# Value products behind both transposes, full-identity column transposes, and a sink column copied by ScalarE, in a hybrid mLSTM and sliding-window layer

## The chip, the core and the metric

The kernel runs on one core of a Trainium2 chip. The metric is the device time in microseconds of one execution, the median of several runs. A core has a matrix engine (TensorE, PE in the profile, with PEld for its weight loads), VectorE (DVE), ScalarE (ACT), GpSimd (POOL), and SyncE (SP), whose queue issues most of the transfers. Each engine takes its instructions in order; instructions of different engines wait for each other by semaphores.

## What is computed

One layer over a prompt of 2048 tokens and a batch of 8 x 16 sample tokens: an input projection, a gated matrix-memory recurrence (mLSTM, 4 heads of 128), sliding-window attention with a learned sink per head (8 query heads, 2 key heads of 64, window of the own chunk of 64 and two before), an output projection with LayerNorm, and a feed-forward part with a causal convolution of width 3. The attention, cut to what matters here:

```python
def band_attend(q, k, v, mask, sinks):
    s = einsum('bnlkgd,bnskd->bnkgls', q, k) * (A_HEAD_DIM ** -0.5)
    s = where(mask, s, -inf)
    sink = sinks.reshape(A_KV_HEADS, A_GROUP)[None, None, :, :, None, None]
    mx = maximum(max(s, axis=-1, keepdims=True), sink)
    p = exp(s - mx)
    p = p / (sum(p, axis=-1, keepdims=True) + exp(sink - mx))
    return einsum('bnkgls,bnskd->bnlkgd', p, v)
```

and of the recurrence, per chunk:

```python
    inter = b + m[..., None]
    dmat = where(causal, b[..., :, None] - b[..., None, :] + li[..., None, :], -inf)
    mt = maximum(inter, max(dmat, axis=-1))
    s = einsum('bhld,bhsd->bhls', qc, kc) * exp(dmat - mt[..., None])
    num = w_inter[..., None] * einsum('bhld,bhde->bhle', qc, C) + einsum('bhls,bhse->bhle', s, vc)
```

## The kernel before

Tokens go in 17 tiles of 128 (16 of the prompt, one of the sample batch). The large products are dense streams on TensorE: the input projection (`i_product`, L704, and `i_direct`, L730), then the output projection (`group`, by `mm3`, L222 to L224), then the two feed-forward products (L1873, L2083). Full precision comes from splitting each operand into a high and a low part and adding three products; the split of weights is a ScalarE cast (L217) and a VectorE subtraction (L218), that of the output projection's input L896 and L897.

The recurrence and the attention of the prompt tiles don't have a stage of their own. They are three generators (`t_sample`, `m_chain`, `a_chain`) whose steps are put between the dense products while the input projection and then the output projection run. TensorE's order is written out in this way by hand; the other engines' orders are found by a scheduler from the program's order and its dependencies.

The planner is `Chains`. Each dense yield adds its cost in ns to a clock `t`. A step yields up to three numbers: its own cost, the delay until the chain may go on, and how many PSUM banks the next step wants. `weave` (L183) takes the next step of a chain when its delay is over and so many of the 5 banks should be free; each bank asked for by `bank` (L927) counts as busy for `HOLDS[name]` ns (L35), or 3500. So a changed number there moves steps of all chains among the dense products.

The attention of one tile (`swa`, L1271): a score step for each half of the heads (`scores`, L1291: products L1303 into psc, mask and row maximum on VectorE, L1307, sink copied into the column behind the scores by GpSimd, L1297), exponentials on ScalarE (L1315, with row sums), division as a reciprocal on VectorE (L1318) and scaling on ScalarE (L1320). Then comes the loop over key tiles kt (nk is 1 for tile 0 and 2 for the others), L1337: eight transposes of the probabilities (L1342 into two ppt banks), copied by ScalarE to pth (L1343), and, one turn of the loop later, the value products of the key tile before (L1348 into ppo, two column halves of 64, one for each key head). In the first turn the next tile's queries and keys are transposed as well (`swa_first`, L1258: pq L1240, pk L1242, splits L217 and L218 to qh, ql, kringh, kringl). At the end ScalarE copies ppo to mixa (L1355) and SyncE stores it.

The recurrence of one tile (`m_tile`, L1182): gate rows (`m_rows`: transposes pgr L1007 and L1008, scans on VectorE, a row M sent through DRAM and broadcast to wi by two GpSimd transfers, L1078 and L1080), a column transpose (`m_cols`, L1020: pcol, 36 rows of ay against a 36x36 identity), exponentials L1117 and L1122, scores (pscore L1128, pkt L1138), then the numerator and state products (pnum L1211 and L1213, pcu L1220). The norm (`m_norm`) is VectorE work from L1150 to L1159 with a copy mr on ScalarE (L1153), a power on GpSimd (L1160), a scaling of hn on ScalarE (L1166, `m_scaled`) and transposes pht (L1176, `m_out`).

`d_sums` (L840) prepares sums of down-projection weights for later in the same stretch: loads into txy, four VectorE operations (L850 to L853), and stores.

Of the kernel before, what the change touches and what calls it, by code (L numbers as in the profile page):

```python
# [14 lines left out]
P = 128  # L15
# [16 lines left out]
RING = 3  # L32

NBANKS = 5
HOLDS = {"pm": 6500, "pgr": 4000, "pnum": 5000, "ppo": 6500}  # L35

WB = 4

# [166 lines left out]
class Prog:  # L205
# [721 lines left out]
    def bank(self, shape, name):  # L927
        self.chains.ask(HOLDS.get(name, 3500))
        return self.tps.tile(shape, F32, name=name, tag="tb")

    def t_setup(self):
        nc, a, tp = self.nc, self.a, self.tp

        def ld(n):
            t = self.one("k_" + n, list(a[n].shape))
            nc.sync.dma_start(t, a[n])
            return t
        nc.sync.dma_start(self.ident, a["ident"])
        self.gb = ld("gb")
        self.mcau = ld("mcau")  # L940
        self.mswa = ld("mswa")
        self.seg = ld("seg")
        self.sink = ld("sink")
        self.sinkx = ld("sinkx")
        self.m0 = ld("m0")
        self.nsink = self.one("nsink", [P, 8])
        nc.vector.tensor_scalar_mul(self.nsink, self.sink, -1.0)
        nc.vector.tensor_scalar_mul(self.sink, self.sink, 8.0)
        self.gm = ld("gm")
        nc.vector.tensor_scalar_mul(self.gm, self.gm, 0.5)  # L950

        raw = self.work("kw", [36, MH])
        nc.sync.dma_start(raw, a["sel"])
        self.sel = self.one("sel", [36, MH], F32R)
        nc.vector.tensor_copy(self.sel, raw)
        self.hl = [self.one(f"hl{i}", [36, P], F32R) for i in range(2)]
        self.ay = [self.one(f"ay{i}", [36, P]) for i in range(2)]
        for i in range(2):
            nc.vector.memset(self.ay[i], 0.0)
            nc.vector.tensor_copy(self.hl[i], self.ay[i])  # L960
        self.kh, self.kl = [self.one(n, [P, RING, P], F32R) for n in ("kringh", "kringl")]
        self.kv = {}
        self.C = self.work("C", [P, MH, 129], bufs=2)
        nc.vector.memset(self.C, 0.0)

        self.M = self.row("M")
        self.mc = self.M[:, P:]
        nc.vector.memset(self.mc, 0.0)
# [51 lines left out]
    def m_cols(self, i):  # L1020

        nc = self.nc
        ps = self.bank([P, 36], "pcol")
        nc.tensor.transpose(ps, self.ay[i], self.ident[:36, :36])
        col = self.work("col", [P, 36], bufs=2)
        nc.vector.tensor_copy(col, ps)
        return col

    def m_emt(self, col):
# [241 lines left out]
    def swa(self, t):  # L1271
        nc = self.nc
        V = nc.vector
        if self.a_first is None:
            self.swa_first(t)
            yield 550, 4000, 2
        qh, ql = self.a_first
        self.a_first = None
        r = t % RING
        if t == 0:  # L1280
            slots, nk = [0], 1
            mask = self.mswa[:, :P]
            sel = slice(0, 1)
        else:
            slots, nk = sorted([(t - 1) % RING, r]), 2
            mask = self.mswa[:, P:] if slots[1] == r else self.mswa[:, :2 * P]
            sel = slice(slots[0], slots[1] + 1, slots[1] - slots[0])
        N = nk * P
        mix = self.work("mixa", [P, 4, P])

        def scores(j0):  # L1291

            sink, nsink = [x.rearrange("p (k j) -> p k j", k=2)[:, :, j0:j0 + 2] for x in (self.sink, self.nsink)]
            sc = self.work("sc", [P, 4, 2 * P + 4], bufs=2)
            mx, sm = [self.work(n, [P, 4], bufs=2) for n in ("amx", "asm")]
            w = lambda x: x.rearrange("p (k j) -> p k j", k=2)
            nc.gpsimd.tensor_copy(sc[:, :, N:N + 1].rearrange("p (k j) o -> p k (j o)", k=2), sink)  # L1297
            ps = [self.bank([P, 2, 2, P], "psc") for _ in range(2)]
            for j in range(2):
                for i, (q, k) in enumerate(((qh, self.kh), (qh, self.kl), (ql, self.kh))):  # L1300
                    for kvh in range(2):
                        rs = slice(64 * kvh, 64 * kvh + 64)
                        nc.tensor.matmul(ps[kvh][:, j, :nk], q[rs, j0 + j], k[rs, sel], start=i == 0, stop=i == 2)  # L1303
            for kvh in range(2):
                for j in range(2):
                    c = 2 * kvh + j
                    V.tensor_tensor_reduce(out=sc[:, c, :N], in0=ps[kvh][:, j, :nk].rearrange("p a b -> p (a b)"), in1=mask, scale=1.0, scalar=-3e38,  # L1307
                                           op0=ALU.add, op1=ALU.max, accum_out=mx[:, c:c + 1])

            V.scalar_tensor_tensor(w(mx), w(mx), -0.125, nsink, op0=ALU.mult, op1=ALU.min)  # L1310
            return sc, mx, sm

        def exps(sc, mx, sm):
            for j in range(4):
                nc.scalar.activation(sc[:, j, :N + 1], sc[:, j, :N + 1], AF.Exp, bias=mx[:, j:j + 1], scale=0.125, accum_out=sm[:, j:j + 1])  # L1315

        def divided(sc, mx, sm):
            V.reciprocal(sm, sm)  # L1318
            for j in range(4):
                nc.scalar.activation(sc[:, j, :N], sc[:, j, :N], AF.Copy, scale=sm[:, j:j + 1])  # L1320

        z = [scores(0)]
        yield 900, 3200, 2
        exps(*z[0])
        z.append(scores(2))
        yield 900, 3600
        exps(*z[1])
        divided(*z[0])
        if t + 1 < NPT and self.i_done > self.place(t + 1)[0]:
            self.a_load = self.swa_dma(t + 1)  # L1330
        yield 0, 3000
        divided(*z[1])
        scs = [x[0] for x in z]
        yield 0, 4200, 2 + 2 * (self.a_load is not None)

        po = pts = None
        for kt in range(nk + 1):  # L1337
            new = self.work("pth", [P, 2, 512], bufs=2) if kt < nk else None
            for kvh in range(2) if kt < nk else ():
                pp = self.bank([P, 512], "ppt")  # L1340
                for j in range(4):
                    nc.tensor.transpose(pp[:, j * P:(j + 1) * P], scs[j // 2][:, 2 * kvh + j % 2, kt * P:(kt + 1) * P], self.ident)  # L1342
                nc.scalar.copy(new[:, kvh], pp)  # L1343
            if kt:
                po = po or self.bank([P, 512], "ppo")
                for kvh in range(2):
                    w = self.kv[slots[kt - 1]][:, P + 64 * kvh:P + 64 * kvh + 64]
                    nc.tensor.matmul(po[64 * kvh:64 * kvh + 64], w, pts[:, kvh], start=kt == 1, stop=kt == nk)  # L1348
            pts = new
            if kt == 0 and self.a_load is not None:  # L1350

                self.swa_first(t + 1)
                self.chains.t += 550
            yield (860 if kt < nk else 0) + (1400 if kt else 0), 0 if kt == nk else 1500 if kt else 3000, 2 * (kt + 1 < nk) + (kt == 0)
        nc.scalar.copy(mix.rearrange("p a b -> p (a b)"), po)  # L1355
        self.mix_out(t, 4, mix)

# [828 lines left out]
```

## Time and profile before

| | us |
|---|---|
| three runs | 2321.00, 2317.24, 2315.28 |
| median | 2317.24 |
| the profiled execution | 2316.15 |
| its span in the trace | 2314.3 |
| mean granted TensorE clock | 0.996 of full speed |

The page gives for each engine the busy time, its share of the span and the number of instructions. A timeline row is start, duration, engine, line, operation, tile written and tiles read, shapes, and the count of instructions merged into the row; in brackets is the time for which the engine stood idle before it and what ended that. A row of a window table has, for a stretch, the busy time of PE, PEld, DVE, ACT and POOL with their instructions, the granted clock, the share of the DMA engines and GB/s. Matmuls overlap, so the distance of their starts counts, not their durations. The prompt tiles' chains run from about 300 to 870 us; up to 640 us the dense stream is the input projection, then it is the output projection.

### The profile page before, as it was taken

How to read it: one execution, taken by the hardware profiler on the slowest of the kernel's cores; microseconds unless marked ns; L12 is line 12 of the kernel's file. 1: busy time of each engine (PE TensorE's matmuls, PEld its weight loads, DVE VectorE, ACT ScalarE, POOL GpSimd, SP SyncE). 2: the span in 40 equal slices, each digit the busy share in tenths (PEclk: the TensorE clock that was granted, in tenths of full speed). 3: DMA queues.
4: the chain of work that ended last, by engine and by line, in shares of the span. 5: the costliest groups of instructions: out<-in, count | busy, mean ns of one | idle time of the engine just before them, and what ended most of it. 6: DMA issues, size and time to landing. Idle time of an engine off the chain costs nothing.

```text
span 2314.3 us, 39788 instructions
## 1 busy us (share of the span) xinstructions
PE 2281.9 (99%) x14293; PEld 2094.9 (91%) x14293; DVE 1808.1 (78%) x3075; ACT 1269.0 (55%) x2377; POOL 279.5 (12%) x509
## 2 busy tenths in 40 slices
PE   8999999999999999999999999999999999999998
PEld 8999989989877778999999999999999978888876
DVE  8777687787688888998788777678766786895987
ACT  5453466776766655555656555555555544444442
POOL 0001000000011212121002000013111200100200
PEclk9999999999999999999999999999999999999999
DMA  7888999999977757888778889978898776756743
GB/s 276 287 308 297 301 309 336 314 310 342 315 269 240 240 201 270 303 319 311 276 289 274 306 304 311 315 264 287 312 294 261 225 282 208 261 175 215 255 157 108
DMA packets 300166, 632.38 MB, mean 273 GB/s; under 512 B 47869, under 2 KB 141121, under 8 KB 299969
## 3 DMA queue, kind: packets, MB, share of 16 engines
q1 hardware_dynamic: 295296, 616.14, 77.9%
q0 software_dynamic: 3520, 10.56, 1.4%
q10 hardware_dynamic: 1152, 3.15, 0.4%
q8 instruction: 113, 1.85, 0.3%
q14 instruction: 85, 0.69, 0.1%
HBM read 458.11 MB, written 171.64 MB: 272 GB/s over the span
## 4 chain that ended last, share of the span: by engine, by line
PE 76%; DVE 5%; DMA 4%; issue 2%; ACT 1%; SPq 0%; POOL 0%; DVEq 0%; ACTq 0%; POOLq 0%
PE dps L1873 19%; PE fup L1873 19%; PE dps L704 7%; PE dps L2083 6%; PE fht L2083 6%; PE fup L2083 6%; PE dps L222 2%; PE dps L224 2%; PE dps L223 2%; PE ppo L1348 1%; PE psc L1303 1%; PE ppt L1342 1%; DVE w L218 1%; PE fht L1697 1%; DMA txy<-wdn 0%
## 5 line engine op out<-in xcount | busy, mean ns | idle before, releaser
L1873 PE MATMUL dps<-hh,uw 128*128 128x384 f32 (+1 forms) x1848 | 478.7, 328 | 2.0 <-DVE u L1904 2.0
L1873 PE MATMUL fup<-hh,uw 128*128 128x384 f32 (+1 forms) x1848 | 478.2, 328 | 1.5 <-ACT ua L1894 1.5
L1873 PEld LDWEIGHTS dps<-hh,uw 128*128 128x128 f32 x1848 | 330.5, 188 | 2.2 <-DVE u L1904 2.2
L1873 PEld LDWEIGHTS fup<-hh,uw 128*128 128x128 f32 x1848 | 330.0, 188 | 2.0 <-ACT ua L1894 1.9
L1930 DVE SCALAR_TENSOR_TENSOR cc<-u,cw,cc 128x768 f32<-128x768 f32 (+1 forms) x264 | 258.1, 978 | 64.9 <-ACT cc L1928 55.5
L1873 PE MATMUL fup<-hl,uw 128*128 128x384 f32 (+1 forms) x924 | 302.5, 327 | 1.7 <-DVE hl L218 1.7
L1873 PE MATMUL dps<-hl,uw 128*128 128x384 f32 (+1 forms) x924 | 302.8, 328 | 0.0
L704 PE MATMUL dps<-w,oh 128*128 128x256 f32 x1344 | 254.3, 284 | 0.7 <-DVE zev L777 0.7
L217 ACT CAST uw<-wraw 128x1024 fp32r<-128x1024 f32 x126 | 123.0, 979 | 223.8 <-PE dps L2083 120.1
L218 DVE TENSOR_TENSOR w<-wraw,w 128x1024 fp32r<-128x1024 f32 (+2 forms) x167 | 189.4, 1141 | 56.1 <-ACT w L217 48.9
L217 ACT CAST w<-wraw 128x1024 fp32r<-128x1024 f32 (+2 forms) x167 | 163.0, 985 | 107.3 <-PE dps L704 38.9
L704 PEld LDWEIGHTS dps<-w,oh 128*128 128x128 f32 x1344 | 210.5, 188 | 11.8 <-issue 8.1
L218 DVE TENSOR_TENSOR uw<-wraw,uw 128x1024 fp32r<-128x1024 f32 x126 | 142.4, 1131 | 65.7 <-ACT uw L217 65.5
L704 PE MATMUL dps<-w,ol 128*128 128x256 f32 x672 | 187.8, 279 | 0.0
L704 PE MATMUL dps<-oh,w 128*128 128x256 f32 x896 | 170.9, 285 | 6.6 <-ACT mr L1153 3.8
L1873 PEld LDWEIGHTS fup<-hl,uw 128*128 128x128 f32 x924 | 173.5, 188 | 2.4 <-DVE hl L218 2.3
L2083 PE MATMUL fup<-uw,fu 128*128 128x512 f32 x726 | 174.2, 396 | 0.6 <-DVE uw L218 0.6
L1873 PEld LDWEIGHTS dps<-hl,uw 128*128 128x128 f32 x924 | 173.8, 188 | 0.0
L2083 PEld LDWEIGHTS fup<-uw,fu 128*128 128x128 f32 x726 | 136.6, 188 | 34.1 <-DVE uw L218 1.1
L2083 PE MATMUL dps<-uw,fu 128*128 128x512 f32 x660 | 165.3, 396 | 1.1 <-DVE uw L218 1.1
L1928 ACT ACTIVATE cc<-u,cw 128x768 f32<-128x768 f32 (+1 forms) x132 | 132.2, 1002 | 57.8 <-DVE u L1910 28.5
L704 PEld LDWEIGHTS dps<-oh,w 128*128 128x128 f32 x896 | 142.2, 191 | 13.1 <-ACT mr L1153 4.1
(318 smaller groups left out, 4567.0 us busy)
## 6 DMA issues: line engine op xcount, KB each, us to landing
uw<-zw SPq DMA_DIRECT2D x176, 512.0 KB, 5.1
zw<-uw SPq DMA_DIRECT2D x88, 512.0 KB, 3.7
w<-zws SPq DMA_DIRECT2D x72, 512.0 KB, 6.2
wv<-wup SPq DMA_DIRECT2D x66, 512.0 KB, 5.0
wraw<-wi SPq DMA_DIRECT2D x65, 512.0 KB, 5.1
wraw<-zt SPq DMA_DIRECT2D x60, 512.0 KB, 4.3
wraw<-wdn SPq DMA_DIRECT2D x45, 512.0 KB, 4.3
wraw<-wo SPq DMA_DIRECT2D x40, 512.0 KB, 4.5
```

The lines of the kernel that those rows point to most:

```text
L217: nc.scalar.copy(hi, src)
L218: nc.vector.tensor_sub(lo, src, hi.bitcast(F32))
L222: mm(out, ah, bh, start=start, stop=False)
L223: mm(out, ah, bl, start=False, stop=False)
L224: mm(out, al, bh, start=False, stop=stop)
L704: mm(o, l, r, start=s in (1, 7) and c == k == i == 0, stop=k == 3 and i == 2, skip_group_check=True)
L1303: nc.tensor.matmul(ps[kvh][:, j, :nk], q[rs, j0 + j], k[rs, sel], start=i == 0, stop=i == 2)
L1342: nc.tensor.transpose(pp[:, j * P:(j + 1) * P], scs[j // 2][:, 2 * kvh + j % 2, kt * P:(kt + 1) * P], self.ident)
L1873: mm(ps, l[:, k], r[:, k], start=s in (1, 7) and k == 0 and i == 0, stop=k == 3 and i == 2, skip_group_check=True)
L1928: S.activation(c[:, v], u[:, 2:2 + n], AF.Identity, bias=w[3], scale=w[2])
L1930: V.scalar_tensor_tensor(c[:, v], u[:, i:i + n], w[i], c[:, v], op0=ALU.mult, op1=ALU.add)
L2083: mm(ps, l[:, k, c], r[:, k], start=s in (1, 4, 7) and u == 0 and k == 0 and i == 0, stop=u == nu - 1 and k == n - 1 and i == 2, skip_grou ...
```

## The change

Three edits. In `m_cols` the column transpose takes all 128 rows of a now 128x128 ay (zero but for the rows used before) against the whole identity, and the copy to col takes the 36 columns that are wanted. In `scores` the sink column is copied by ScalarE, after the row maxima, in place of GpSimd before the score products. In the loop over key tiles the value products come in one step behind the transposes of both key tiles, with other yields; and the planner's hold for ppo is 5000 in place of 6500.

```diff
-HOLDS = {"pm": 6500, "pgr": 4000, "pnum": 5000, "ppo": 6500}
+HOLDS = {"pm": 6500, "pgr": 4000, "pnum": 5000, "ppo": 5000}
...
-        self.ay = [self.one(f"ay{i}", [36, P]) for i in range(2)]
+        self.ay = [self.one(f"ay{i}", [P, P]) for i in range(2)]
         for i in range(2):
             nc.vector.memset(self.ay[i], 0.0)
-            nc.vector.tensor_copy(self.hl[i], self.ay[i])
+            nc.vector.tensor_copy(self.hl[i], self.ay[i][:36])
...
-        ps = self.bank([P, 36], "pcol")
-        nc.tensor.transpose(ps, self.ay[i], self.ident[:36, :36])
+        ps = self.bank([P, P], "pcol")
+        nc.tensor.transpose(ps, self.ay[i], self.ident)
         col = self.work("col", [P, 36], bufs=2)
-        nc.vector.tensor_copy(col, ps)
+        nc.vector.tensor_copy(col, ps[:, :36])
...
-            nc.gpsimd.tensor_copy(sc[:, :, N:N + 1].rearrange("p (k j) o -> p k (j o)", k=2), sink)
             ps = [self.bank([P, 2, 2, P], "psc") for _ in range(2)]
...
             V.scalar_tensor_tensor(w(mx), w(mx), -0.125, nsink, op0=ALU.mult, op1=ALU.min)
+            nc.scalar.copy(sc[:, :, N:N + 1].rearrange("p (k j) o -> p k (j o)", k=2), sink)
             return sc, mx, sm
...
-        po = pts = None
-        for kt in range(nk + 1):
-            new = self.work("pth", [P, 2, 512], bufs=2) if kt < nk else None
-            for kvh in range(2) if kt < nk else ():
+        pts = []
+        for kt in range(nk):
+            new = self.work("pth", [P, 2, 512], bufs=2)
+            for kvh in range(2):
                 pp = self.bank([P, 512], "ppt")
                 for j in range(4):
                     nc.tensor.transpose(pp[:, j * P:(j + 1) * P], scs[j // 2][:, 2 * kvh + j % 2, kt * P:(kt + 1) * P], self.ident)
                 nc.scalar.copy(new[:, kvh], pp)
-            if kt:
-                po = po or self.bank([P, 512], "ppo")
-                for kvh in range(2):
-                    w = self.kv[slots[kt - 1]][:, P + 64 * kvh:P + 64 * kvh + 64]
-                    nc.tensor.matmul(po[64 * kvh:64 * kvh + 64], w, pts[:, kvh], start=kt == 1, stop=kt == nk)
-            pts = new
+            pts.append(new)
             if kt == 0 and self.a_load is not None:
 
                 self.swa_first(t + 1)
                 self.chains.t += 550
-            yield (860 if kt < nk else 0) + (1400 if kt else 0), 0 if kt == nk else 1500 if kt else 3000, 2 * (kt + 1 < nk) + (kt == 0)
+            yield 860, 3000 if kt + 1 == nk else 1500, 1 if kt + 1 == nk else 2
+        po = self.bank([P, 512], "ppo")
+        for kt in range(nk):
+            for kvh in range(2):
+                w = self.kv[slots[kt]][:, P + 64 * kvh:P + 64 * kvh + 64]
+                nc.tensor.matmul(po[64 * kvh:64 * kvh + 64], w, pts[kt][:, kvh], start=kt == 0, stop=kt + 1 == nk)
+        yield 1400 * nk, 0
         nc.scalar.copy(mix.rearrange("p a b -> p (a b)"), po)
```

## The prediction

> **What bounds the kernel now.** I read the page's span and engine shares first, then who TensorE waited for in the stretch in which attention and the gated recurrence run (300 to 870 us), then TensorE, ScalarE and VectorE in order of time around the steps that the change touches.
>
> ```profile
> span 2314.3 us, 39788 instructions
> PE 2281.9 (99%) x14293; PEld 2094.9 (91%) x14293; DVE 1808.1 (78%) x3075; ACT 1269.0 (55%) x2377; POOL 279.5 (12%) x509
> ```
>
> TensorE is busy 99% of the span; it sets the time. A microsecond counts only if it is TensorE's own work or a gap in TensorE. Its gaps in that stretch are few:
>
> ```profile
> PE dps L704 <- ACT mr L1153: 3.8, 1, 3.8
> PE ppt L1342 <- ACT pth L1343: 1.6, 1, 1.6
> PE pht L1176 <- DVE ql L218: 1.0, 1, 1.0
> PE ppo L1348 <- ACT pth L1343: 0.6, 1, 0.6
> ```
>
> (columns: total us, times, longest). So there is about 7 us to win in gaps, and whatever the step's own products lose when they interrupt the dense stream.
>
> **TensorE's own work: packing the value products and padding the column transpose.** In order of time, a dense product starts every 0.23 us; what a step costs is the time from the last dense start before it to the second dense start after it, less two such intervals (0.47).
>
> ```profile
> 661.72 0.40 PE L224 MATMUL dps<-w,ol 128*128 128x512 f32 x1
> 662.05 0.25 PE L1024 MATMUL pcol<-ident,ay 36*128 36x36 f32 x1
> 662.23 1.08 PE L1348 MATMUL ppo<-pth,kva 128*64 128x512 f32 x4
> 663.58 0.39 PE L223 MATMUL dps<-w,oh 128*128 128x512 f32 x1
> ```
> ```profile
> 761.46 0.39 PE L223 MATMUL dps<-w,oh 128*128 128x512 f32 x1
> 761.69 0.40 PE L224 MATMUL dps<-w,ol 128*128 128x512 f32 x1
> 762.02 0.25 PE L1024 MATMUL pcol<-ident,ay 36*128 36x36 f32 x1
> 762.53 0.39 PE L223 MATMUL dps<-w,oh 128*128 128x512 f32 x1
> 762.76 0.40 PE L224 MATMUL dps<-w,ol 128*128 128x512 f32 x1
> 763.09 1.08 PE L1348 MATMUL ppo<-pth,kva 128*64 128x512 f32 x4
> 764.44 0.39 PE L223 MATMUL dps<-w,oh 128*128 128x512 f32 x1
> ...
> 766.47 0.40 PE L224 MATMUL dps<-w,ol 128*128 128x512 f32 x1
> 766.70 0.27 PE L1007 MATMUL pgr<-ident,g 128*4 128x128 f32 x1
> 767.16 0.39 PE L223 MATMUL dps<-w,oh 128*128 128x512 f32 x1
> ```
> ```profile
> 791.29 0.40 PE L224 MATMUL dps<-w,ol 128*128 128x512 f32 x1
> 791.53 1.04 PE L1342 MATMUL ppt<-ident,sc 128*128 128x128 f32 x8
> 792.49 1.08 PE L1348 MATMUL ppo<-pth,kva 128*64 128x512 f32 x4
> 793.50 0.50 PE L222 MATMUL dps<-w,oh 128*128 128x512 f32 x1
> 793.84 0.40 PE L223 MATMUL dps<-w,oh 128*128 128x512 f32 x1
> ```
>
> A column transpose alone: 762.53 - 761.69 - 0.47 = 0.37 us, though it streams only 36 columns. Value products of one key tile alone: 764.44 - 762.76 - 0.47 = 1.21. Both together: 663.58 - 661.72 - 0.47 = 1.39. Eight transposes with products behind: 793.84 - 791.29 - 0.47 = 2.08, so the transposes take 2.08 - 1.21 = 0.87. The two gate transposes, all 128 rows deep: 767.16 - 766.47 - 0.47 = 0.22, or 0.11 each.
>
> Before, a tile of tokens with two key tiles pays 2.08 + 1.39 = 3.47. After, it pays 0.87 for the second transposes, one column transpose and one group of both key tiles' products. The 128x128 column transpose I take at 0.11, the gate transposes' price; its other end is its old 0.37. The double group the trace doesn't show. Between transposes and dense work, one key tile took 793.50 - 792.49 = 1.01, so I take 1.21 + 1.01 = 2.22. Its ends are 2.42 (nothing saved) and 2.02 (it sheds the 0.20 between 1.21 and 1.01 a second time). Sum after 0.87 + 0.11 + 2.22 = 3.20: 0.27 saved, for the 15 tiles with two key tiles **-4.1 us** (from -7.1 to -1.1). Tile 0 and the sample batch keep one group; their transposes add under 0.6.
>
> A page of the Trainium skill speaks against the padding: TensorEngine Tiling (Array Packing), under Instruction Overhead, has each matmul cost about as much as 60 columns, so 128 columns instead of 36 would cost some 68 cycles more, an estimate from that page of under 1 us over the 17 transposes, in place of a gain. The same page, under Key Properties, says that a change of tiling mode drains TensorE; the row of 0.37 us for 36 rows beside 0.11 for 128 agrees with that second rule, and I go by the row.
>
> **An early gap that goes.** Once, VectorE stood at a weight sum whose load was late, with the statistics that release TensorE's next bank behind it:
>
> ```profile
> 325.20 0.69 DVE L850 TENSOR_TENSOR txy<-txy 128x512 f32<-128x512 f32 x1 [3.92 <-DMA txy<-wdn]
> 325.81 0.29 DVE L1150 BATCH_NORM_STATS2 bst<-pnum 128x6 f32<-128x128 f32 x1
> ```
> ```profile
> 330.30 0.58 PE L704 MATMUL dps<-oh,w 128*128 128x256 f32 x1 [3.85 <-ACT mr L1153]
> ```
> ```profile
> 326.00:330.00 4.00, 0.46 (x4) 0.24 (x3) 3.85 (x16) 1.37 (x3) 0.00 (x0) 0.98 0.78 231
> 330.00:334.00 4.00, 3.70 (x20) 3.70 (x21) 4.00 (x10) 2.86 (x9) 0.00 (x0) 0.59 1.09 333
> ```
>
> (windows: PE, PEld, DVE, ACT, POOL busy, then granted clock.) ScalarE's mr waits for L1150, and the copy that frees TensorE's bank stands behind mr. TensorE lost 3.85 us, and in the next 4 us its clock was 0.59: 0.41 x 4 = 1.6 more. In the changed kernel as built, VectorE's order at this place has L850 behind the whole chain L1150 to L1159, some 6 us later, when the load (landed by 325.2) is there. Nothing that TensorE needs stands behind it then. **-5.4 us**; the other end is 0, if the load meets something else.
>
> The Trainium skill, TensorE: Matmul & The Clock Gate, Part 1, says that an idle window of about 3.4 us halves the clock until a busy one has passed; the row with 0.59 agrees.
>
> The other three gaps (1.6 + 1.0 + 0.6) sit at pairs of steps which the change pulls apart or re-times; I take them as gone, **-3.2 us** (or 0).
>
> **What becomes late: the second half's division.** The steps' waits and bank needs are new, and so the planner puts them in another order. In the output-projection stage (640 to 870 us) the second score step now comes 15 dense products before the recurrence's numerator, where it came 30 before. Its division is therefore issued after the recurrence's norm. As built, in three of the tiles of that stage VectorE's reciprocal L1318 stands behind L1159, and ScalarE's scaling L1320 behind the norm's L1166, which waits for GpSimd. The first transposes of the probabilities need all four of these scalings. One such tile in the old order, with pnum at 745.65:
>
> ```profile
> 745.65 0.39 PE L1211 MATMUL pnum<-v,dt 128*128 128x129 f32 x2
> ```
> ```profile
> 754.84 0.16 DVE L1159 TENSOR_TENSOR mr<-mr,bmv 128x4 f32<-128x4 f32 x1
> ```
> ```profile
> 755.15 1.89 POOL L1160 TENSOR_TENSOR ms<-mr,mhalf 128x4 f32<-128x4 f32 x1 [6.48 <-DVE mr L1159]
> ```
> ```profile
> 753.19 1.04 PE L1342 MATMUL ppt<-ident,sc 128*128 128x128 f32 x8
> ```
> ```profile
> 746.67 1.71 ACT L1320 ACTIVATE sc<-sc,asm 128x256 f32<-128x256 f32 x4
> ...
> 757.08 1.28 ACT L1166 ACTIVATE hn<-hn,ms 128x128 f32<-128x128 f32 x4 [1.52 <-POOL ms L1160]
> ```
>
> The norm ended at 758.36, 12.7 after pnum. Four scalings (1.71) bring that to 14.4. The transposes are due 7.54 after pnum now and, with 15 more dense products between (15 x 0.23 = 3.5), 11.0 then; the eight would end at 11.7. A gap of 14.4 - 11.7 = 2.7. A later tile, with pnum at 812.37, sets the far end:
>
> ```profile
> 823.37 0.16 DVE L1159 TENSOR_TENSOR mr<-mr,bmv 128x4 f32<-128x4 f32 x1
> ```
>
> There L1159 came 11.0 after pnum against 9.2, so 4.5. I take 2.9 for each of three tiles, and 1.0 for one weight cast that stands between norm and scaling in one of them: **+9.7 us**, from 0 (scalings in time) to 14.5. Behind a gap here, all dense products wait, nothing else becomes late.
>
> In three others the norm is followed on ScalarE by up to three weight casts and only then by the copies of the probabilities. Such a run:
>
> ```profile
> 648.65 3.18 ACT L217 CAST w<-wraw 128x1024 fp32r<-128x1024 f32 x3
> ```
>
> 12.7 + 3.2 + 0.6 for a copy = 16.5 after pnum, while the column transpose that reuses the copied bank is due at 11.0 + 1.4 (transposes and the next tile's loads) + 12 x 0.23 + 0.4 = 15.6. **+3 us** in all, from 0 to 6.
>
> **The sink column.** 32 copies of 128x4 leave GpSimd for ScalarE. The nearest row there, an exponential of the same size:
>
> ```profile
> 662.56 0.20 ACT L1031 ACTIVATE emt<-col 128x4 f32<-128x4 f32 x1 [0.67 <-DVE col L1026]
> ```
>
> 0.2 us each, 0.4 a tile, in a queue that is 55% busy; in the built order they stand behind the copies that drain the second transposes, so that they wait for nothing late. I cost them at nothing; without that cover, in the same queue as the late scalings, they cost 32 x 0.2 = 6.4. On GpSimd, L1558 and the recurrence's two transfers lose an instruction ahead of them that waited for transposes; no gap of TensorE named those. The store of the attention output is issued some 2 us later in SyncE's queue; its reader is a later block. The zeroing of larger ay tiles happens once.
>
> **The sum** against the profiled execution's own 2316.15 us: -4.1 - 5.4 - 3.2 + 9.7 + 3.0 = 0.0. The median of the runs shown is 2317.24, 1.1 higher, well inside their spread. I forecast **2316 us**, no change; of this kernel 0.3% (7 us) is about what a measurement can tell from none.
>
> **The rivals.** (1) Faster: VectorE reaches L1159 sooner, as it has more dense time around it, and neither division nor copies are late. Then 2316.15 - 12.7 = 2303. For it: the sooner end of L1159 isn't bounded by TensorE. Against: the chain takes weight casts in between in every tile I looked at. (2) Slower: each of the three late divisions costs the 4.5 of the far row and, as a gap over 3.8 us did before, 1.6 us of halved clock; with 1 for the cast and 6 for the others: -12.7 + 3 x 6.1 + 7 = +12.6, 2329. It decides from L1159 at 11 us after pnum on. (3) The packing and padding do nothing: the double group costs 2.42, the padded transpose 0.37, so a tile pays 3.66, 0.19 more than now: +2.9 in place of -4.1, 2323. Against it stand the 1.01 and 0.11 rows.
>
> **How the numbers follow.** My forecast 0.53, (1) 0.25, (2) 0.16, (3) 0.06. Case (1) gives faster; (2) and a part of (3) give slower: faster 0.26, within 0.3% 0.54, slower 0.20. The forecast's own range, with the bounds of its terms, is 2309 to 2322. The range 2302 to 2326 takes in (1) and (3) and leaves out most of (2).
>
> **What would show it.** In the profile after: column transposes 128x128 costing 0.1 us; eight value-product records together in about 2.2; no gap at 326 us and no 0.59 clock behind it; in the waits, PE ppt L1342 on ACT sc (the scalings) with 5 to 14 us in total, all after 640 us. If that wait is missing, (1) holds and I am wrong by the whole 9.7; if the granted clock drops behind these waits, (2).

## The result and the profile after

| | before | changed |
|---|---|---|
| runs | 14 | 14 |
| median, us | 2316.36 | 2321.34 |
| lowest and highest, us | 2312.09, 2324.22 | 2314.04, 2324.79 |

The ratio is 1.0018, with a 95% interval of 1.0010 to 1.0027: slower by 4 us (2317.24 x 0.0018), less than the 7 us set as the bound of no change, but more than its interval. The changed kernel's profiled execution took 2314.04 us, the lowest of its 14. A second one, e1_again below, took 2320.04 and stands near the median, so the account of times uses both.

The page of the changed kernel, first lines:

```profile
span 2312.2 us, 39714 instructions
...
PE 2276.4 (98%) x14293; PEld 2093.5 (91%) x14293; DVE 1808.9 (78%) x3075; ACT 1270.4 (55%) x2409; POOL 268.0 (12%) x477
```

TensorE still sets the time, and again the gaps decide. Its waits from 300 to 870 us (columns: total us, times, longest):

```profile
PE ppt L1342 <- ACT sc L1320: 4.8, 2, 4.5
PE pht L1176 <- ACT hn L1166: 1.3, 3, 0.5
PE pnum L1211 <- issue: 1.3, 1, 1.3
```

These are the first three of ten rows. The wait for mr (3.8) and the wait for pth of 1.6 are gone; the late scalings that the prediction named head the list, but with one wait of 4.5 where it had three of 2.9. (Lines from 1302 on have moved by one or a few: the norm keeps L1150 to L1166, the value products are L1354.)

**TensorE's own work.** The changed kernel's timeline of TensorE, a double group of value products and a full column transpose:

```profile
716.90 0.27 PE L1024 MATMUL pcol<-ident,ay 128*128 128x128 f32 x1
717.01 1.03 PE L1342 MATMUL ppt<-ident,sc 128*128 128x128 f32 x8
...
721.36 0.39 PE L224 MATMUL dps<-w,ol 128*128 128x512 f32 x1
721.67 1.94 PE L1354 MATMUL ppo<-pth,kva 128*64 128x512 f32 x8
723.54 0.50 PE L222 MATMUL dps<-w,oh 128*128 128x512 f32 x1
723.88 0.40 PE L223 MATMUL dps<-w,oh 128*128 128x512 f32 x1
```

The column transpose takes 717.01 - 716.90 = 0.11 us, the double group 723.88 - 721.36 - 0.47 = 2.05. With 0.87 for the transposes a tile pays 3.03 where it paid 3.47, so 15 tiles save 6.6 us; this is an estimate from these rows, and the other undisturbed groups of the trace repeat them within 0.02 us.

**The early gap.** The changed kernel's VectorE, then TensorE's waits from 300 to 345 us, then its windows (PE, PEld, DVE, ACT, POOL busy, granted clock, DMA share, GB/s):

```profile
330.07 0.15 DVE L1159 TENSOR_TENSOR mr<-mr,bmv 128x4 f32<-128x4 f32 x1
330.14 0.68 DVE L850 TENSOR_TENSOR txy<-txy 128x512 f32<-128x512 f32 x1
```
```profile
307.05 0.33 PE L1302 MATMUL psc<-kringl,qh 64*128 64x128 f32 x2 [0.73 <-DVE kringl L218]
318.64 1.13 PE L1211 MATMUL pnum<-v,dt 128*128 128x129 f32 x8 [1.29 <-issue]
332.22 0.33 PE L1176 MATMUL pht<-ident,hn 128*128 128x128 f32 x1 [0.39 <-ACT hn L1166]
332.99 0.33 PE L1176 MATMUL pht<-ident,hn 128*128 128x128 f32 x1 [0.45 <-ACT hn L1166]
333.81 0.62 PE L1176 MATMUL pht<-ident,hn 128*128 128x128 f32 x2 [0.48 <-ACT hn L1166]
```
```profile
330.00:334.00 4.00, 2.68 (x19) 2.05 (x17) 2.90 (x6) 2.24 (x7) 1.36 (x1) 1.00 1.04 396
334.00:338.00 4.00, 4.00 (x21) 3.89 (x20) 2.77 (x5) 4.00 (x11) 0.00 (x0) 0.57 0.92 305
```

L850 stands behind L1159 and no longer waits, as foretold. But the five brackets add up to 3.3 us. The kernel before had the first two waits as well, though smaller: 0.26 us ahead of its numerator at 319.2 us, and for the keys

```profile
308.75 0.33 PE L1303 MATMUL psc<-kringl,qh 64*128 64x128 f32 x2 [0.50 <-DVE kringl L218]
```

With its gap of 3.85 that is 4.6 us, so the waits of this stretch fell by 1.3 us, not by 3.85. And 4 us with a clock of 0.57 come here too, only later.

**The late division.** The prediction's three tiles: the start of the numerator, L1159, the last scalings, and the transposes that need them, each from the changed kernel's timeline of that engine:

```profile
668.07 0.38 PE L1211 MATMUL pnum<-v,dt 128*128 128x129 f32 x2
...
679.09 1.31 PE L1342 MATMUL ppt<-ident,sc 128*128 128x128 f32 x8
...
734.12 0.38 PE L1211 MATMUL pnum<-v,dt 128*128 128x129 f32 x2
...
745.90 1.13 PE L1342 MATMUL ppt<-ident,sc 128*128 128x128 f32 x5 [0.33 <-ACT sc L1320]
...
801.50 0.38 PE L1211 MATMUL pnum<-v,dt 128*128 128x129 f32 x2
...
812.52 0.38 PE L1342 MATMUL ppt<-ident,sc 128*128 128x128 f32 x2
817.39 1.73 PE L1342 MATMUL ppt<-ident,sc 128*128 128x128 f32 x6 [4.49 <-ACT sc L1320]
```
```profile
675.73 0.16 DVE L1159 TENSOR_TENSOR mr<-mr,bmv 128x4 f32<-128x4 f32 x1
...
741.90 0.15 DVE L1159 TENSOR_TENSOR mr<-mr,bmv 128x4 f32<-128x4 f32 x1
...
813.37 0.15 DVE L1159 TENSOR_TENSOR mr<-mr,bmv 128x4 f32<-128x4 f32 x1
```
```profile
816.83 1.71 ACT L1320 ACTIVATE sc<-sc,asm 128x256 f32<-128x256 f32 x4
```

The transposes are due 11.0 us after pnum in all three (679.09 - 668.07, 812.52 - 801.50), as worked out. L1159 comes 7.7, 7.8 and 11.9 us after pnum, so two tiles lose 0 and 0.33, and the third 4.49. In the third, two of the eight transposes run on time, as they need none of the late scalings, and TensorE goes on as soon as the first of the four is done. Around that gap the clock falls:

```profile
816.00:820.00 4.00, 2.61 (x12) 2.31 (x13) 3.32 (x3) 3.59 (x7) 0.00 (x0) 0.50 0.89 271
820.00:824.00 4.00, 4.00 (x16) 3.15 (x16) 2.81 (x7) 1.59 (x6) 0.42 (x1) 0.69 0.62 231
```

The clock record has one stretch of 6.8 us at half speed here, from 815.7 us. Its first 1.7 us fall into the gap, where TensorE stands anyway; the 5.1 us behind the gap cost at most 2.6 us.

**Where the time went.** The start of the same dense product, found in both traces by its number in the stream, shows how far the changed kernel is ahead or behind. Differences against the profile before, by stretches of that profile; the third line is the 15 tiles' saving. The fourth is the gap with its half clock; it is measured against e5 below, whose TensorE runs the same instructions in the same order and waits only 0.55 us there. The two profiles lose 5.8 and 7.2 us against e5 in that stretch; with e5's 0.55 these are the values given:

```
us                          after (2314.04)   e1_again (2320.04)
0 to 50                          -2.9               +0.1
50 to 870, of this:              +1.9               +0.8
  value products, transposes     -6.6               -6.6
  gap at 818 and its clock       +6.3               +7.7
  all else                       +2.2               -0.3
870 to 960                       +2.2               +4.0
960 to the end                   -3.2               -1.0
sum                              -2.0               +3.9
```

The first line is the chance of the clock: the profile before has two stretches at half clock in its first 50 us (granted 0.93 there), e1_again has them too, the other profile has none (1.00). Of the +2.2 in "all else", 1.2 lie ahead of 300 us. The line 870 to 960, the first steps of the feed-forward part, nobody had foreseen.

### The profile page after: what moved, and what is told of

Same layout as the page of the kernel before. It is cut to its first block, busy times and chain, and to the rows that moved or that the text cites. A ratio compares the mean times of both kernels' runs of the same rounds, so it can differ in the third digit from the quotient of the medians.

```text
span 2312.2 us, 39714 instructions
## 1 busy us (share of the span) xinstructions
PE 2276.4 (98%) x14293; PEld 2093.5 (91%) x14293; DVE 1808.9 (78%) x3075; ACT 1270.4 (55%) x2409; POOL 268.0 (12%) x477
## 4 chain that ended last, share of the span: by engine, by line
PE 73%; DVE 6%; DMA 4%; ACT 2%; issue 2%; POOL 0%; SPq 0%; DVEq 0%; ACTq 0%; POOLq 0%
PE dps L1874 19%; PE fup L1874 19%; PE dps L2084 6%; PE fht L2084 6%; PE fup L2084 6%; PE dps L704 5%; PE dps L222 2%; PE dps L223 2%; PE dps L224 2%; DMA r<-zf 1%; PE ppt L1342 1%; PE ppo L1354 1%; DVE w L218 1%; DMA txy<-wdn 1%; ACT sc L1315 1%
## 5 line engine op out<-in xcount | busy, mean ns | idle before, releaser
L2084 PEld LDWEIGHTS dps<-uw,fu 128*128 128x128 f32 x660 | 123.9, 188 | 31.4 <-DVE uw L218 1.5
```

The costliest lines, as they stand in the source:

```text
L2084: mm(ps, l[:, k, c], r[:, k], start=s in (1, 4, 7) and u == 0 and k == 0 and i == 0, stop=u == nu - 1 and k == n - 1 and i == 2, skip_grou ...
```

## The experiments

Each stands beside runs of the kernel before on the same chip (medians 2316.4 to 2317.5 us). Theory D is the prediction's: the late division sets the gap at 818 us.

**e1: the changed kernel once more**, no edit, for a second profile.

> The changed kernel once more, for the trace of another execution. Theory D (late divisions: in three tiles of the output-projection stage ScalarE's scaling of the second score half stands behind the recurrence's norm): 2321 us again, and in an execution near that time the gaps of TensorE at the first probability transposes before ACT sc L1320 sum to 6 to 12 us after 640 us, with stretches of halved clock behind them (the profiled execution of 2314.04 had 4.8). Rival E (the time is lost elsewhere, in the feed-forward stage or at the start): these gaps stay at 5 us or less and the time stands at another place.

2319.99 us, ratio 1.0014 (1.0004 to 1.0024). The slowdown holds. The gap at 818 us is 5.34 us here, and with one of 0.34 the waits for scalings come to 5.7, just short of the 6 that D asked for. The mean granted clock of the 12 runs is 0.9950, of the 35 runs before 0.9959: 0.0009 x 2317 = 2.1 us of a mean difference of 3.1. So up to two thirds of the slowdown are time at half clock.

**e2: the second half's division first, in every tile.**

```diff
-        divided(*z[1])
+        with self.tc.high_priority():
+            divided(*z[1])
```

> The changed kernel with the second division issued at high priority, so that its reciprocal and its scalings stand ahead of the norm on VectorE and ScalarE; TensorE's order is unchanged. D: no wait of ppt for ACT sc above 1 us, 5 to 10 us faster than the changed kernel, 2311 to 2316 us. E: within 2 us of the changed kernel, 2319 to 2323.

2319.82 us, ratio 1.0008 (0.9995 to 1.0020), where D had 2311 to 2316. The wait for scalings is gone, the gap isn't. TensorE's waits of this run, 600 to 880 us:

```profile
PE pht L1176 <- ACT hn L1166: 7.3, 2, 6.5
```

The norm itself is now the late thing. So D in its simple form, that the order of division and norm is all, fell.

**e3: the column transposes alone, on the kernel before.**

```diff
-        self.ay = [self.one(f"ay{i}", [36, P]) for i in range(2)]
+        self.ay = [self.one(f"ay{i}", [P, P]) for i in range(2)]
...
-        nc.tensor.transpose(ps, self.ay[i], self.ident[:36, :36])
+        nc.tensor.transpose(ps, self.ay[i], self.ident)
```

> The kernel before with only the 128x128 column transposes. Its order of instructions on VectorE has the weight sum L850 behind the statistics at the place of the early gap, as in the changed kernel. My pricing: column transposes save 13 x 0.07 + 3 x 0.26 = 1.7 us, the gap of 3.85 us at 330 us and its 1.6 us of lost clock go: 2309 to 2313 us. Rival (128 columns in place of 36 cost more, and the gap comes back elsewhere): 2316 to 2318.

2315.36 us, ratio 0.9987 (0.9972 to 1.0001): 3 us faster in the middle, not certain, and between the two expectations. The early gap of 3.85 is gone here already, and the small waits for norms (1.3 us) stand in its place as in the changed kernel.

**e4: the value products alone, on the kernel before.**

```diff
-HOLDS = {"pm": 6500, "pgr": 4000, "pnum": 5000, "ppo": 6500}
+HOLDS = {"pm": 6500, "pgr": 4000, "pnum": 5000, "ppo": 5000}
...
+        po = self.bank([P, 512], "ppo")
+        for kt in range(nk):
+            for kvh in range(2):
+                w = self.kv[slots[kt]][:, P + 64 * kvh:P + 64 * kvh + 64]
+                nc.tensor.matmul(po[64 * kvh:64 * kvh + 64], w, pts[kt][:, kvh], start=kt == 0, stop=kt + 1 == nk)
+        yield 1400 * nk, 0
```

> The kernel before with only the value products behind both transposes, their yields and the hold of 5000; the sink stays on GpSimd, the column transpose at 36 rows. D: it has late divisions in four tiles and keeps the early gap, so it is slower than the changed kernel, 2322 to 2328 us. Rival S (the sink copies on ScalarE cost the time): faster than the changed kernel by 4 to 7, 2314 to 2317.

2323.52 us, ratio 1.0031 (1.0021 to 1.0042). The cheaper products alone make the kernel slower by 6 us, with the wait for scalings (4.8 us) and the early wait (3.3 us) both there.

**The theory after these.** In the tile of the gap, ScalarE has another instruction out of place. The changed kernel's ScalarE, then SyncE's issues:

```profile
786.32 0.19 ACT L1310 COPY sc<-k_sink 128x4 f32<-128x4 f32 x1
793.42 1.05 ACT L896 CAST oh<-xraw 128x1024 fp32r<-128x1024 f32 x1 [6.92 <-DMA xraw<-zmix]
794.38 0.58 ACT L1356 COPY mixa<-ppo 128x512 f32<-128x512 f32 x1
794.85 0.20 ACT L1310 COPY sc<-k_sink 128x4 f32<-128x4 f32 x1
798.37 0.51 ACT L1315 ACTIVATE sc<-sc,amx 128x257 f32<-128x257 f32 x1 [3.32 <-DVE amx L1309]
```
```profile
783.51 0.38 SPq L1170 DMA_DIRECT2D zmix<-mixm  x1
...
789.42 0.89 SPq L892 DMA_DIRECT2D xraw<-zmix  x2
```

The cast reads a block of mixes that the store at 783.51 completes; store and load take till 793.4. In the changed kernel the cast stands ahead of mixa and the exponentials; in the kernel before it stands behind them (801.73 and 804.64 us in the profile before). That the scheduler moved it because mixm comes earlier is likely, but not shown. VectorE stands too, at ol, the subtraction behind the cast (3.0 us). Theory X: this wait makes the tile late. Rival N: the gap is repaid elsewhere.

**e5: that one cast behind the exponentials.**

```diff
-        nc.scalar.copy(h, raw)
+        with self.tc.issue_after(self.exp_done) if (b, p) == (3, 0) else nullcontext():
+            nc.scalar.copy(h, raw)
...
-                nc.scalar.activation(sc[:, j, :N + 1], sc[:, j, :N + 1], AF.Exp, bias=mx[:, j:j + 1], scale=0.125, accum_out=sm[:, j:j + 1])
+                self.exp_done = nc.scalar.activation(sc[:, j, :N + 1], sc[:, j, :N + 1], AF.Exp, bias=mx[:, j:j + 1], scale=0.125, accum_out=sm[:, j:j + 1]).ins
```

> The changed kernel with one edge more: ScalarE's cast oh<-xraw of the output projection's fourth block (tokens 10 to 13, the first of its four casts) is held behind the exponentials of tile 14's first half. ScalarE's order up to that tile is the changed kernel's own. Theory X (the cast at the head of ScalarE's queue waits for the store of tile 13's mix and the load behind it, 5.9 + 4 us, with mixa and the exponentials behind it): the wait on xraw<-zmix ahead of the cast falls from 6.7-6.9 us to under 1, the TensorE gap of 4.5 to 5.3 us at 818 us and the 6.8 us window at half clock behind it are gone, and the time is 2320 less 5.0 less 3.4, about 2311 to 2314. Rival D (the second half's late division sets the gap): this tile's division also moves ahead of the norm here, so D too expects the gap gone; the next run tells them apart. Rival N (the gap is repaid by slack later, or the time lies elsewhere): gap gone, time 2318 to 2322 as before.

2311.96 us, ratio 0.9984 (0.9973 to 0.9996): faster than both kernels. The scheduler, given the edge, also put all four scalings ahead of the norm in this tile, so two things changed at once. L1159 came 11.9 us after pnum, no sooner than in the changed kernel. One wait of half a microsecond is left there:

```profile
818.50 1.21 PE L1177 MATMUL pht<-ident,hn 128*128 128x128 f32 x4 [0.55 <-ACT hn L1167]
```

**e6: all casts of that kind behind the exponentials** (the same edit without its condition).

> The changed kernel with each of the output projection's input casts (x_pair, all blocks) held behind the exponentials last emitted. In the tile at 818 us the cast now comes after the first half's exponentials, while three of the second half's four scalings still stand behind the norm, as in the changed kernel. Theory X: the gap at 818 us is gone (under 1 us), no half clock there, 2311 to 2315. Rival D (the late division): the gap stays at 4 to 5 us on ppt waiting for the scalings, 2318 to 2322. Elsewhere the edge changes the order of a few scalings, worth under 2 us either way.

2320.49 us, ratio 1.0020 (1.0008 to 1.0033): no gain, against X. TensorE's waits for scalings:

```profile
747.32 1.27 PE L1343 MATMUL ppt<-ident,sc 128*128 128x128 f32 x5 [2.41 <-ACT sc L1321]
...
815.54 0.33 PE L1343 MATMUL ppt<-ident,sc 128*128 128x128 f32 x1 [0.64 <-ACT sc L1321]
818.63 1.27 PE L1343 MATMUL ppt<-ident,sc 128*128 128x128 f32 x5 [2.76 <-ACT sc L1321]
```

In the old place the cast is behind and the division late: 0.64 + 2.76 = 3.4 us remain, which D alone makes. The edge moved other work in the tile at 747 us, where L1159 came 9.9 us after pnum in place of 7.8, and that tile, harmless until then, lost 2.41.

**e7: the sink copied by GpSimd again, in the changed kernel** and **e8: that, with the edge of e6.**

```diff
+            nc.gpsimd.tensor_copy(sc[:, :, N:N + 1].rearrange("p (k j) o -> p k (j o)", k=2), sink)
...
-            nc.scalar.copy(sc[:, :, N:N + 1].rearrange("p (k j) o -> p k (j o)", k=2), sink)
```

> The changed kernel with the sink column copied by GpSimd again, at the place it had before; value products and column transposes as changed. Theory X: the cast stands at the same place ahead of mixa and the exponentials, so the gap at 818 us stays at 4 to 6 us and the time is that of the changed kernel, 2318 to 2322. Rival S (32 copies of 0.2 us on ScalarE and their places cost part of the loss): 2313 to 2317, with ScalarE's exponentials in the score steps 0.4 us sooner and the gap under 4.

> The edge of the run before last (casts behind the exponentials) and the sink on GpSimd together. If the two edits do not meet, the time is that of the casts held behind alone within 2 us: 2311 to 2315 by theory X. If the sink column on ScalarE costs something by itself, 2 to 4 us below that. By D it stays at 2318 to 2322.

2321.53 us, 1.0024 (1.0011 to 1.0037), with a gap of 4.4, as X expected; and 2324.23, 1.0038 (1.0025 to 1.0051), above all that was expected of it. Neither is faster with the sink on GpSimd: that edit is not where the time went.

**e9: the value products alone with the one edge of e5**, and **e10: e5 once more.**

> The kernel before with the merged value products alone (as in e4_products) and the one edge of e5_cast_last: the first cast of the output projection's fourth block behind the exponentials of tile 14's first half. Theory X2 (two causes at one place: with that cast ahead the tile at 818 to 830 us has a gap of 4.4 to 6.5 us whichever way the division is ordered; with the cast behind it, 2.8 us where the division is late and under 0.6 where it isn't): here the cast is behind and the division ahead of the norm, so the gap of 4.79 us at 827 us goes, with its 3.4 us of half clock: 2323.5 less 8 = 2313 to 2317. The early gap at 330 us stays at 3.3 us. Rival N (chance of one chip): 2320 to 2326, as e4_products.

> The kernel of e5_cast_last once more, on the chip of this call. Theory X2: 2310 to 2314, 3 to 6 us under before, no TensorE gap over 1 us between 600 and 880 us. If its first result was chance: 2316 to 2320.

2315.76 us, 0.9989 (0.9977 to 1.0001), where e4 had 1.0031: one edge is worth 0.0042 x 2317 = 10 us. And 2310.55 us, 0.9978 (0.9967 to 0.9990): e5's gain holds, 5 us below before.

**e11: the sink on ScalarE alone, on the kernel before** (e7's edit the other way).

> The kernel before with the sink column copied by ScalarE behind the score step's minimum, alone. ScalarE's order of the exponentials, scalings, norms and casts is that of before in all 16 tiles. Expected: the time of before within 2 us, the gap at 330 us still there, no gap over 2 us between 600 and 880. Rival S (the copies on ScalarE cost): 3 to 6 us above before.

2317.88 us, ratio 1.0000 (0.9989 to 1.0011). The sink copies cost nothing that shows; the 3 us at least of rival S lie outside the interval. One detail missed: a wait of 2.5 us for pth at 658 us, 1.65 in the profile before.

**e12: the division first in tile 14 alone**, in the changed kernel; the cast stays ahead.

```diff
-        divided(*z[1])
+        with self.tc.high_priority() if t == 14 else nullcontext():
+            divided(*z[1])
```

> The changed kernel with the second half's division raised in priority in tile 14 alone: ScalarE's four scalings move ahead of the recurrence's norm in the one tile with the gap, the cast stays ahead of mixa and the exponentials, and nothing earlier on ScalarE changes place. Theory X2 (with the cast ahead the gap comes whichever way the division is ordered): a gap of 4 to 6.5 us near 818 us, now on the norm (pht waiting for hn) in place of the scalings, and 2317 to 2322. Rival D (the late division alone): no gap over 1 us there, 2310 to 2314, as e5_cast_last.

2315.94 us, ratio 1.0002 (0.9992 to 1.0011): between the two expectations. The gap came as X2 said, on the norm. TensorE, GpSimd and VectorE of this run:

```profile
828.97 1.35 PE L1176 MATMUL pht<-ident,hn 128*128 128x128 f32 x4 [6.14 <-ACT hn L1166]
```
```profile
823.20 5.27 POOL L1160 TENSOR_TENSOR ms<-mr,mhalf 128x4 f32<-128x4 f32 x1 [9.93 <-DVE mr L1159]
```
```profile
822.90 0.16 DVE L1159 TENSOR_TENSOR mr<-mr,bmv 128x4 f32<-128x4 f32 x1
822.98 1.22 DVE L218 TENSOR_TENSOR w<-wraw,w 128x1024 fp32r<-128x1024 f32 x1
824.11 1.22 DVE L897 TENSOR_TENSOR ol<-xraw,oh 128x1024 fp32r<-128x1024 f32 x1
825.25 1.22 DVE L218 TENSOR_TENSOR w<-wraw,w 128x1024 fp32r<-128x1024 f32 x1
826.38 1.22 DVE L897 TENSOR_TENSOR ol<-xraw,oh 128x1024 fp32r<-128x1024 f32 x1
```

But the number has another make-up than X2 had it. In e5 L1159 came 11.9 us after pnum and the GpSimd step took 1.87; here 14.1 and 5.27. That is 2.2 + 3.4 = 5.6, the whole difference of 6.14 and 0.55. Only the first part can be the cast's wait. The second comes from four subtractions in a row on VectorE, where e5 has two over that step; whether the cast's place led to that order isn't shown.

**What the four kinds together say of the tile at 818 us** (TensorE's gap, us):

| | division late | division ahead of the norm |
|---|---|---|
| cast ahead of the exponentials | 4.5, 5.3 (changed), 4.8 (e4), 4.4 (e7) | 6.5 (e2), 6.1 (e12) |
| cast behind them | 3.4 (e6, e8; two waits) | 0.55 (e5, e9, e10) |

With the division late, the cast ahead adds 1.0 to 1.9, and about 3.4 is the division's. With the division early and the cast ahead there are 6 us, 3.4 of them by a longer GpSimd step. Neither remedy alone takes the gap away; together they do.

The stretch 870 to 960 us goes with the division, not the cast: the six profiles with tile 14's division late (both of the changed kernel, e4, e6, e7, e8) lose 2.1 to 4.0 us there against before, the five with it early (e2, e5, e9, e10, e12) gain 0.8. The waits named are for feed-forward weights, in e1_again:

```profile
909.84 0.50 PE L1863 MATMUL fup<-hh,uw 128*128 128x512 f32 x1 [0.92 <-ACT uw L217]
912.50 0.63 PE L1874 MATMUL fup<-hh,uw 128*128 128x384 f32 x2 [1.80 <-DVE uw L218]
```

One step further back, VectorE's sums of these weights (uw, L1792) wait 3.3 to 4.3 us for the load of wg in the six, at most 0.7 in the five (1.5 before). That load is issued at the same place of the dense stream in all of them, but lands only after 6.0 to 8.0 us in the six, after 3.1 to 3.4 in the five. Ahead of it in SyncE's queue, two loads of output-projection weights are issued some 4 us later in the six. What holds these two up wasn't followed; that remains open. So does why e8 is the slowest.

## Why the prediction was nearly right, and where it was wrong

The forecast was 2316 us, no change, and the kernel came out slower by 0.18%: inside the 7 us, yet more than the measurement's interval leaves to chance. By the steps of the sum:

- **TensorE's work, -4.1.** Right in kind, too small: the double group took 2.05, the value of its lower bound 2.02, not 2.22; -6.6. The padded column transpose cost 0.11, as taken. Rival (3) fell.
- **The early gap, -5.4, and three others, -3.2.** This is the step that failed. L850 went behind L1159 and the gap went, exactly as described. But the credit assumed that no other wait would grow. The wait for the keys grew from 0.50 to 0.73, that for the numerator from 0.26 to 1.29, and 1.3 us of waits for the scaled hn are new, so that 1.3 of the 3.85 us were won. The 1.6 us of clock weren't won in either profile, as a stretch at half clock stands there again; that part was chance, for e5, e6, e7, e8 and e10 have the same five waits, within 0.15 us each, and none. The stretch 300 to 345 us gained 1.2 and 1.3 us in the two profiles, a share of the -6.6 included. With the small gaps, "all else" is +2.2 and -0.3 where the sum had -8.6 + 3.0 = -5.6. Why the numerator's wait grew isn't known.
- **The late division, +9.7.** The mechanism, the tiles and the time at which the transposes are due were right; the size of each was not. L1159 at 9.2 us after pnum was one tile's row set for three. Two had 7.7 and 7.8, and the third was the tile of the prediction's own far row, 11.0 before and 11.9 now. That it lost just the 4.5 worked out for that end is luck: L1159 came 0.9 later, GpSimd's step took 1.01 where the working had 1.89, a weight cast of 1.0 stood between norm and scalings, and TensorE needed the first scaling to go on, not all four. With the half clock, which only rival (2) counted, the total is 6.3 and 7.7; that it lies within 3.4 us of 9.7 comes from errors that cancel. That a cast ahead in the queue adds 1 to 2 us to it wasn't seen at all.
- **The late copies, +3.0.** Not there: the changed kernel waits for pth once, 0.6 us.
- **The sink column, 0.** Right within the measurement (e11: ratio 1.0000, 0.9989 to 1.0011; e7).
- **Not in the sum:** 2.2 and 4.0 us at the start of the feed-forward part.

So the terms in e1_again's profile are -6.6 + 7.7 - 0.3 + 4.0 - 1.0 + 0.1 = +3.9, where the sum had 0.0. That the number still came within 5 us is luck: most of a credit of 8.6 failed, and a larger saving and late copies that never came made up for a part of it. Rival (1)'s condition held in two tiles of three, rival (2)'s in one, clock and all. A version that has the change's saving and not its gap exists: e5 is 0.16% and, measured again, 0.22% faster than before.

## What to carry to other kernels

A wait that vanishes is worth less than its length when other waits around it grow, here 1.3 of 3.85 us: list what else is due in the same few microseconds before crediting it, and credit no clock unless all gaps there go. When a reordering puts work behind an uneven chain, take the chain's time from each tile's own row; one slow tile held nearly all of the loss that three were thought to share. Where instructions have been moved among in-order queues, look also for a read of a fresh store at a queue's head; here one edge on one cast, with the order that followed from it, was worth 7 to 10 us.

## What the runs showed of the hardware

**GpSimd's small power step is stretched by VectorE's wide subtractions.** The same 128x4 step took 1.0 us where VectorE ran other work, 1.87 in e5, 3.4 us in one tile of the changed kernel and 5.27 in e12, where four subtractions of 128x1024 ran back to back over it (rows above: it ends 0.9 us after the last of them). Which of the two starts first seems to decide: in e12 the step began 0.22 us after a subtraction; at 774.55 us in the changed kernel it began 0.07 us ahead of one, and took 1.04. The Trainium skill, SBUF — State Buffer, under Who interferes with whom, has an instruction of VectorE with two SBUF inputs contend with a GpSimd instruction that reads SBUF; the rows agree, and they add that four in a row can hold it off for over 4 us.

**Half clock comes in fixed stretches, at the mercy of phase.** The clock records show stretches of 3.4 or 6.8 us, nothing between, but for the one at the span's end. A gap of 4.49 us in the changed kernel and one of 6.14 in e12 each came with a stretch of 6.8 us; 5.1 us of it lay behind the gap in the first and 2.9 in the second (825.1 to 831.9 us, the gap's end at 828.97). The gap of 2.41 us in e6 (747.32 above) had one of 3.4 right behind it, the same gap of 2.42 in e8 had none, so the 3.4 us of idle time that the prediction cites were not needed here. The page TensorE: Matmul & The Clock Gate of the Trainium skill, Part 1, calls the window free-running, which fits. It also fits the spread of one kernel's runs: the fastest of the changed kernel's 14 (2314.04 us) has a granted clock of 0.997, the slowest (2324.79) 0.993, and 0.004 x 2320 = 9 us of the 11 between them.
